# A hybrid decoder layer in float32: products and sums from GpSimd to VectorE, and the DeltaNet decay chain between two tiles of the RG-LRU

## The chip, the cores and the metric

The kernel runs on one core of a Trainium2 chip. The metric is the device time of one execution in microseconds, the median of several runs. Before the change it is 1122.11 us, the median of 3 runs (1121.78 to 1124.39).

## What is computed

One layer (depth 1) of a recurrent decoder, for a prompt of 512 tokens and 8 samples of 8 tokens, 576 columns together; the model width is 1024. Cut to what matters here:

```
h = rmsnorm(x); proj = h @ w_in
rg_x, rg_gate, s5_u, qkv, z, a_in, b_in, gate_logits = split(proj)
y_rg = (linear_scan(a, inp) * gelu(rg_gate)) @ w_o          # RG-LRU, width-4 conv before it
y_s5 = glu(gelu(Re(C s) + D u)) @ w_o                       # complex diagonal state space
# gated DeltaNet, 4 heads of 128: width-4 conv, silu, normed q and k
g    = -exp(a_log) * softplus(a_in + dt_bias); beta = sigmoid(b_in)
gc   = cumsum(g) in each chunk; decay = exp(gc_i - gc_j)
T    = inverse(I + strict(beta k k^T * decay)); u = T (beta v); w = T (beta k exp(gc))
v_new = u - w S; o = (q exp(gc)) S + (q k^T * decay) v_new; S = S exp(g_last) + k_dec^T v_new
y_gd = (rmsnorm(o) * silu(z)) @ w_o
mixed = sum_b sigmoid(gate_b) * y_b
x = x + rmsnorm(mixed @ w_out)
x = x + rmsnorm((silu(hf @ w_gate) * (hf @ w_up)) @ w_down),  hf = rmsnorm(x)
```

The outputs are y and the new states of the three branches, for the prompt and for each sample.

## The kernel before

All activations lie transposed, features on the 128 partitions and the 576 columns free, in two halves of 288. Each large product is made of three passes in a reduced format: weights and activations are split into a high and a low part, and high·high, high·low and low·high are summed in PSUM (`mm_part`, lines L199, L200, L201; in the last stage L1379 to L1381). A weight piece of 128x512 comes from HBM into `wr` (two buffers, line L170, on SP's queue), ACT makes its high part `wh` (L181), VectorE its low part `wl` (L182); four buffers of each. Activations are split in the same way (L236, L237).

The program is a list of tiles written in Python; a scheduler gives every engine its order of instructions, by the order in which they are written and by when buffers and operands are free in its own timeline. Each engine then works through its queue in that order and waits at each instruction for what it needs. Buffers matter: the big products go through three PSUM buffers `mm`, small ones through three `sm` and two `sr`; gates, merges and squares through a pool `T`; the 512 KB of sample states of a head, `s0` (`s` in the profile), through one buffer, so that the load of the next head's (L1159, SP's queue) follows the store of the one before (L1187).

The stages in order, with the names that the steps below use:

- The first norm and its split into `hh`, `hl` (line L374 in the second half); S5's tables and chunks (`s5_front`, `s5_chain`; products L699 and L700 into `s5yp`); the four tiles of the RG-LRU (`rg`), each with a convolution (L420 is one tap of such a convolution, L407 ACT's copy into the padded tile `pad`).
- Merge gates (`gate`, L788) and merges (`merge`): product with the branch's output weights, times the gate (L802, into `mg` or `mt`), from the second branch on added to the sum `mg` (L804, 128x576 on GpSimd). S5's GLU adds its parts in L822.
- The decay chain: a projection to 16 rows (`abps`, L849), transposes (`abc`), softplus and exponentials in some 50 small VectorE operations up to `gcl` (L871), cumulative sums on PE (`gcps`, L873 to L878), `bgp` (L901), a way through HBM (`bgd`).
- DeltaNet, two heads at a time: q, k, v (`gdn_qkv`, its `sqp` L931), `gdn_prep` (decay matrices `dt`, L973 to L983, products `kp` L994), `gdn_blk` (the inverse of 16x16 blocks by 15 steps on VectorE; L1032, L1036, L1064, L1067), `gdn_inv` (larger blocks by products `yp`, `pp`; L1078, L1081), `gdn_run` (the prompt's chunks, `tps`, `stp`, VectorE's `vk` L1124), `gdn_smp` (the samples: `zq` L1165, `s0` times the decay L1166, `zt` L1168, transposition L1169, `rrs` L1171, product L1172, `vns` L1174, L1175, masked copies `vm` L1180, product `up` L1183, sum L1184) and `gdn_outs` (norms of the heads: `cps`, L1197, the steps of a reciprocal root L112 to L118, `rows` L1204, L1206).
- After the last merge (gdn_wo), the product with w_out and its norm (squares summed in L1288, residual sum L1305), the feed-forward with 22 blocks (`ar`, L1331), and the last norm (squares summed in L1437, L1441 the scaled product, L1442 the residual sum, L1443 the output's DMA, eight of each in a half).

The scheduled order around the change is set by where the tiles are written:

Of the kernel before, what the change touches and what calls it, by code (L numbers as in the profile page):

```python
# [18 lines left out]
NT = 576  # L19
# [46 lines left out]
def hybrid_step(ctx: ExitStack, tc: tile.TileContext, i, o, dbg=None):  # L66
# [304 lines left out]
    def x_h(half):  # L371
        for k in range(KT):
            t = R("h")[:, :NH]
            (G if half and k % 4 == 3 else V).tensor_tensor(t, xa[:, k, hsl(half)], rw_[half], op=OP.mult)  # L374
            split(t, h[k][0][:, hsl(half)], h[k][1][:, hsl(half)])
# [415 lines left out]
    def merge(name, b, y, perm=False, ms=range(8), gates=()):  # L791
        for m in ms:
# [10 lines left out]
            if b:  # L803
                G.tensor_tensor(acc[m], acc[m], dst[:, :NT], op=OP.add)  # L804
# [5 lines left out]
    def s5_glu():  # L810
# [5 lines left out]
        for m in range(4):  # L816
# [5 lines left out]
            G.tensor_tensor(y[:, :NT], yh.bitcast(F32), yo.bitcast(F32), op=OP.add)  # L822
# [10 lines left out]
    rg_h = [rg(m) for m in range(3)]  # L833
    rg_h.append(rg(3))
    g1 = [gate(0, m) for m in range(5)]
# [70 lines left out]

    DQ.dma_start(o["rg_h"], hout)
# [56 lines left out]
    def gdn_prep(hd, st_):  # L964
# [14 lines left out]
        G.tensor_tensor(dt, dt, tri[:, None, :].to_broadcast([128, 4, 128]), op=OP.mult)  # L979
        G.tensor_tensor(dts, dts, C("tris")[:64], op=OP.mult)  # L980
        bt4 = bet[:, 0:NP].rearrange("p (n c) -> p n c", n=4)
        G.tensor_tensor(bt4, bt4, dt, op=OP.mult)
        G.tensor_tensor(bet[:64, NP:NT], bet[:64, NP:NT], dts, op=OP.mult)  # L983
# [25 lines left out]
        G.tensor_tensor(kqe[:, 1, :], kqe[:, 1, :], eg, op=OP.mult)  # L1009
# [14 lines left out]
    def gdn_blk(hds):  # L1024
# [3 lines left out]
        for e, hd in enumerate(hds):  # L1028
# [3 lines left out]
            G.tensor_tensor(t, st_["nq"][:, :, 0, :].rearrange("p n (b f) -> p n b f", f=16),  # L1032
# [3 lines left out]
            G.tensor_tensor(ts, st_["nqs"][:, 0, :].rearrange("p (b f) -> p b f", f=16),  # L1036
# [20 lines left out]
        for e, hd in enumerate(hds):  # L1057
# [9 lines left out]
            G.tensor_tensor(st_["nqs"][:, 0, :].rearrange("p (b f) -> p b f", f=16),  # L1067
# [6 lines left out]
    def gdn_inv(hd):  # L1074
# [3 lines left out]
        G.tensor_tensor(nl, nmat, lvl[:, None, :].to_broadcast([128, 4, 128]), op=OP.mult)  # L1078
# [77 lines left out]
    def gdn_smp(hd, st_):  # L1156
# [9 lines left out]
        G.tensor_tensor(s0, s0, egls[:, hd, :, None].to_broadcast([128, 8, 128]), op=OP.mult)  # L1166
# [11 lines left out]
        for a in range(2):  # L1178
            vm = GG("vm", 4, 128)[:64]
            G.tensor_tensor(vm, vn[:, None, :].to_broadcast([64, 4, 128]),  # L1180
# [102 lines left out]
    def add_sq(name, ss, src, last):  # L1283
# [4 lines left out]
        (V if last else G).tensor_tensor(ss, ss, sq, op=OP.add)  # L1288
        return ss

    for half in range(2):
# [10 lines left out]
        for m in range(8):  # L1302
            xv = x1[m][:, sl]
            V.scalar_tensor_tensor(xv, xv, P("g_post")[:, m:m + 1], rows, op0=OP.mult, op1=OP.mult)
            (V if m in (5, 7) else G).tensor_tensor(xv, xv, xr[m][:, sl], op=OP.add)  # L1305
# [117 lines left out]
    for half in range(2):  # L1423
        sl = hsl(half)
        prev, marks[:] = marks[:], []
        for m in range(KT):
# [9 lines left out]
            elif m < 7:  # L1436
                (V if half and m > 3 else G).tensor_tensor(ss, ss, sq, op=OP.add)  # L1437
        rows = norm_rows(tp2, [ss, sq], 1.0 / D, 4 * EPS)
        for m in range(8):
            xv = mx[m][:, sl]  # L1440
            V.scalar_tensor_tensor(xv, xv, P("g_postff")[:, m:m + 1], rows, op0=OP.mult, op1=OP.mult)  # L1441
            (V if half and m in (3, 5, 7) else G).tensor_tensor(xv, xv, x1[m][:, sl], op=OP.add)  # L1442
# [141 lines left out]
```

## Time and profile before

| | |
|---|---|
| median of 3 runs | 1122.11 us (1121.78 to 1124.39) |
| profiled execution | 1126.14 us |
| its span | 1124.4 us, 20031 instructions |
| TensorE's granted clock, mean | 0.974 |
| PE, VectorE, ACT, GpSimd busy | 1065.3, 714.6, 414.6, 176.9 us |
| HBM traffic | 89.05 MB read, 8.24 MB written |

The profiled execution is one of the program on the chip. Its span runs from the first to the last recorded instruction; the execution's own time is some 1.7 us longer. A busy time is what the engine's instructions took; a wait is put down to the instruction that ended last before it. PEclk is the granted clock of TensorE as a share of full speed, 1.0 or 0.5 at any one time.

### The profile page before, as it was taken

The page shows a single profiled execution, that of the slowest core. Times are in us where ns is not written, and L with a number is a line of the kernel's source. Part 1 is how long each engine was busy: PE and PEld are TensorE (multiplying, and loading weights), DVE is VectorE, ACT ScalarE, POOL GpSimd, SP SyncE. Part 2 cuts the span into 40 slices and gives each one's busy share as a digit, 9 for nine tenths or more (in the row PEclk, how much of TensorE's full clock was granted, in tenths as well). Part 3 has the DMA queues.
Part 4 walks back from the last instruction along what each step waited for, and adds up shares of the span by engine and source line. Part 5 has one row for each costly group of instructions (what it writes and reads, how often), then busy time and mean ns, then how long its engine had stood idle before and what let it go on. Part 6 is the DMA issues. An engine that isn't in the chain of part 4 may idle for free.

```text
span 1124.4 us, 20031 instructions
## 1 busy us (share of the span) xinstructions
PE 1065.3 (95%) x7874; PEld 1019.3 (91%) x7874; DVE 714.6 (64%) x1698; ACT 414.6 (37%) x847; POOL 176.9 (16%) x247
## 2 busy tenths in 40 slices
PE   6999999968999999999999998999999999999995
PEld 4899989967989889997989998899999999999994
DVE  8899989858977688546358377552344344443346
ACT  4368843425434432222334353343322222322211
POOL 1012111204532252221004231000000000000014
PEclk9999999978999999999999999999999999999997
DMA  6323224331322242222113514142222322213002
GB/s 199 107 83 101 79 80 110 91 93 53 111 86 79 84 136 63 74 95 76 57 53 122 178 57 131 57 146 80 77 94 76 94 76 82 87 57 94 1 1 85
DMA packets 61744, 98.59 MB, mean 88 GB/s; under 512 B 26570, under 2 KB 34898, under 8 KB 61650
## 3 DMA queue, kind: packets, MB, share of 16 engines
q1 hardware_dynamic: 61650, 97.31, 28.2%
q8 instruction: 62, 1.02, 0.4%
q14 instruction: 32, 0.26, 0.1%
HBM read 89.05 MB, written 8.24 MB: 87 GB/s over the span
## 4 chain that ended last, share of the span: by engine, by line
PE 82%; DVE 10%; DMA 4%; issue 2%; ACT 2%; POOL 0%; SPq 0%; DVEq 0%; ACTq 0%
PE mm L199 19%; PE mm L201 19%; PE mm L200 19%; PE mm L1381 4%; PE mm L1379 4%; PE mm L1380 4%; PE mm L381 2%; DVE wl L182 2%; DMA xa<-in_x 1%; PE up L1183 1%; PE rows L262 1%; PE gps L748 1%; PE s5yp L700 1%; DVE bu L1053 1%; PE s5yp L699 1%
## 5 line engine op out<-in xcount | busy, mean ns | idle before, releaser
L182 DVE TENSOR_TENSOR wl<-wr,wh 128x512 fp32r<-128x512 f32 x268 | 195.5, 734 | 171.9 <-ACT wh L181 164.9
L181 ACT ACTIVATE wh<-wr 128x512 fp32r<-128x512 f32 x268 | 166.3, 629 | 375.1 <-PE mm L200 226.4
L199 PE MATMUL mm<-hh,wh 128*128 128x288 f32 x768 | 233.0, 304 | 6.7 <-ACT pad L407 5.4
L200 PE MATMUL mm<-hl,wh 128*128 128x288 f32 x768 | 231.4, 301 | 0.0
L201 PE MATMUL mm<-hh,wl 128*128 128x288 f32 x768 | 230.1, 300 | 0.0
L199 PE MATMUL mm<-hfh,wh 128*128 128x288 f32 x704 | 208.7, 297 | 2.3 <-DVE ar L1331 1.9
L201 PE MATMUL mm<-hfh,wl 128*128 128x288 f32 x704 | 208.5, 297 | 0.0
L200 PE MATMUL mm<-hfl,wh 128*128 128x288 f32 x704 | 208.1, 296 | 0.0
L199 PEld LDWEIGHTS mm<-hh,wh 128*128 128x128 f32 x768 | 145.9, 190 | 12.7 <-ACT pad L407 5.6
L201 PEld LDWEIGHTS mm<-hh,wl 128*128 128x128 f32 x768 | 146.1, 190 | 2.8 <-issue 2.2
L200 PEld LDWEIGHTS mm<-hl,wh 128*128 128x128 f32 x768 | 146.1, 190 | 2.5 <-issue 1.7
L199 PEld LDWEIGHTS mm<-hfh,wh 128*128 128x128 f32 x704 | 133.5, 190 | 2.7 <-DVE ar L1331 2.2
L200 PEld LDWEIGHTS mm<-hfl,wh 128*128 128x128 f32 x704 | 133.6, 190 | 0.2 <-DVE hfl L237 0.2
L201 PEld LDWEIGHTS mm<-hfh,wl 128*128 128x128 f32 x704 | 133.4, 190 | 0.0
L1381 PE MATMUL mm<-fh,wl 128*128 128x288 f32 x352 | 104.0, 295 | 0.0
L1379 PE MATMUL mm<-fh,wh 128*128 128x288 f32 x320 | 94.5, 295 | 0.0
L1380 PE MATMUL mm<-fl,wh 128*128 128x288 f32 x320 | 94.3, 295 | 0.0
L199 PE MATMUL mm<-brh,wh 128*128 128x288 f32 x224 | 67.4, 305 | 4.3 <-DVE mg L802 1.9
L1437 POOL TENSOR_TENSOR fs<-fs,fs 128x288 f32<-128x288 f32 x9 | 7.3, 806 | 400.9 <-ACT fs L1433 400.9
L200 PE MATMUL mm<-brl,wh 128*128 128x288 f32 x224 | 68.2, 305 | 0.9 <-DVE brl L237 0.6
L201 PE MATMUL mm<-brh,wl 128*128 128x288 f32 x224 | 66.9, 299 | 0.0
L1381 PEld LDWEIGHTS mm<-fh,wl 128*128 128x128 f32 x352 | 66.1, 188 | 0.0
(464 smaller groups left out, 1905.5 us busy)
## 6 DMA issues: line engine op xcount, KB each, us to landing
wr<-in_w_in SPq DMA_DIRECT2D x48, 512.0 KB, 3.6
wr<-in_w_gate SPq DMA_DIRECT2D x22, 512.0 KB, 3.5
wr<-in_w_up SPq DMA_DIRECT2D x22, 512.0 KB, 3.6
wr<-in_w_down SPq DMA_DIRECT2D x20, 512.0 KB, 3.6
wr<-in_w_out SPq DMA_DIRECT2D x8, 512.0 KB, 3.5
xa<-in_x SPq DMA_DIRECT2D x8, 288.0 KB, 6.2
xr<-in_x SPq DMA_DIRECT2D x4, 576.0 KB, 8.1
out_y<-xr SPq DMA_DIRECT2D x16, 144.0 KB, 1.8
```

The lines of the kernel that those rows point to most:

```text
L181: S.activation(hi, raw, AF.Copy)
L182: (eng or lo_eng()).tensor_tensor(lo, raw, hi.bitcast(F32), op=OP.subtract)
L199: PE.matmul(acc, hi[:, k, :], xh[:, sl], start=k0 + k == 0, stop=False)
L200: PE.matmul(acc, hi[:, k, :], xl[:, sl], start=False, stop=False)
L201: PE.matmul(acc, lo[:, k, :], xh[:, sl], start=False, stop=k0 + k == n - 1)
L262: m0 = PE.matmul(rows[:, 96 * b:96 * b + 96], rc[:96, b:b + 1].to_broadcast([96, 128]), ident[:96, :96], start=True, stop=True).ins
L381: PE.matmul(ps, uw[m][k], xa[:, k, hsl(half)], start=k == 0, stop=k == KT - 1)
L699: PE.matmul(ypv[:, b_, :], tm[:, g, :], x[:, g, :], start=True, stop=False)
L700: PE.matmul(ypv[:, b_, :], cl[g // 4][:, g % 4, 1:9, :].rearrange("p d h -> p (d h)"), st[:, g, :], start=False, stop=True)
L1379: PE.matmul(acc, hi[:, k0 + k, :], xh, start=k == 0, stop=False)
L1380: PE.matmul(acc, hi[:, k0 + k, :], xl, start=False, stop=False)
L1381: PE.matmul(acc, lo[:, k0 + k, :], xh, start=False, stop=k == len(x) - 1)
```

## The change

116 operations of two tensors (17 lines) go from GpSimd to VectorE: the split norm product (L374), the merge sums (L804), S5's GLU sum (L822), DeltaNet's masks and decays (L979 to L983, L1009, L1032, L1036, L1067, L1078), the samples' decay and masked copies (L1166, L1180), and the sums of the later norms (L1288, L1305, L1437, L1442). GpSimd keeps copies and memsets. And the tiles of the RG-LRU are written in two pairs, with the decay chain between them and the first merge gates behind the second pair. Each line of the new kernel from here on has a number up to two lower than before (the decay chain) or the same. Cut to the lines that change:

```diff
@@ -371,7 +371,7 @@
     def x_h(half):
...
             t = R("h")[:, :NH]
-            (G if half and k % 4 == 3 else V).tensor_tensor(t, xa[:, k, hsl(half)], rw_[half], op=OP.mult)
+            V.tensor_tensor(t, xa[:, k, hsl(half)], rw_[half], op=OP.mult)
...
     def x_u(half, m, after=None):
@@ -801,7 +801,7 @@
...
             if b:
-                G.tensor_tensor(acc[m], acc[m], dst[:, :NT], op=OP.add)
+                V.tensor_tensor(acc[m], acc[m], dst[:, :NT], op=OP.add)
@@ -819,7 +819,7 @@
...
             yh, yo = yl[m]
-            G.tensor_tensor(y[:, :NT], yh.bitcast(F32), yo.bitcast(F32), op=OP.add)
+            V.tensor_tensor(y[:, :NT], yh.bitcast(F32), yo.bitcast(F32), op=OP.add)
@@ -830,9 +830,7 @@
...
     DQ.dma_start(o["s5"], s5o)
-    rg_h = [rg(m) for m in range(3)]
-    rg_h.append(rg(3))
-    g1 = [gate(0, m) for m in range(5)]
+    rg_h = [rg(m) for m in range(2)]
@@ -904,6 +902,8 @@
...
+    rg_h += [rg(m) for m in range(2, 4)]
+    g1 = [gate(0, m) for m in range(5)]
@@ -976,11 +976,11 @@
...
         S.activation(eg, eg, AF.Exp)
-        G.tensor_tensor(dt, dt, tri[:, None, :].to_broadcast([128, 4, 128]), op=OP.mult)
-        G.tensor_tensor(dts, dts, C("tris")[:64], op=OP.mult)
+        V.tensor_tensor(dt, dt, tri[:, None, :].to_broadcast([128, 4, 128]), op=OP.mult)
+        V.tensor_tensor(dts, dts, C("tris")[:64], op=OP.mult)
         bt4 = bet[:, 0:NP].rearrange("p (n c) -> p n c", n=4)
-        G.tensor_tensor(bt4, bt4, dt, op=OP.mult)
-        G.tensor_tensor(bet[:64, NP:NT], bet[:64, NP:NT], dts, op=OP.mult)
+        V.tensor_tensor(bt4, bt4, dt, op=OP.mult)
+        V.tensor_tensor(bet[:64, NP:NT], bet[:64, NP:NT], dts, op=OP.mult)
@@ -1006,7 +1006,7 @@
...
         V.tensor_tensor(nqs[:, 1], kpv[:, 1], dts, op=OP.mult)
-        G.tensor_tensor(kqe[:, 1, :], kqe[:, 1, :], eg, op=OP.mult)
+        V.tensor_tensor(kqe[:, 1, :], kqe[:, 1, :], eg, op=OP.mult)
@@ -1029,11 +1029,11 @@
...
             t = GG("nl", 4, 8, 16)
-            G.tensor_tensor(t, st_["nq"][:, :, 0, :].rearrange("p n (b f) -> p n b f", f=16),
+            V.tensor_tensor(t, st_["nq"][:, :, 0, :].rearrange("p n (b f) -> p n b f", f=16),
...
             ts = gp.tile([64, 4, 16], F32, name=nm("cms"), tag="cms")
-            G.tensor_tensor(ts, st_["nqs"][:, 0, :].rearrange("p (b f) -> p b f", f=16),
+            V.tensor_tensor(ts, st_["nqs"][:, 0, :].rearrange("p (b f) -> p b f", f=16),
@@ -1064,7 +1064,7 @@
...
                                 bd[:, None, :, None].to_broadcast([128, 4, 8, 16]), op=OP.mult)
-            G.tensor_tensor(st_["nqs"][:, 0, :].rearrange("p (b f) -> p b f", f=16),
+            V.tensor_tensor(st_["nqs"][:, 0, :].rearrange("p (b f) -> p b f", f=16),
@@ -1075,7 +1075,7 @@
...
         nl = GG("nl", 4, 128)
-        G.tensor_tensor(nl, nmat, lvl[:, None, :].to_broadcast([128, 4, 128]), op=OP.mult)
+        V.tensor_tensor(nl, nmat, lvl[:, None, :].to_broadcast([128, 4, 128]), op=OP.mult)
@@ -1163,7 +1163,7 @@
...
             PE.matmul(zqv[:, b], s0[:, b, :], kqe[:, :, c0:c0 + 8], start=True, stop=True)
-        G.tensor_tensor(s0, s0, egls[:, hd, :, None].to_broadcast([128, 8, 128]), op=OP.mult)
+        V.tensor_tensor(s0, s0, egls[:, hd, :, None].to_broadcast([128, 8, 128]), op=OP.mult)
@@ -1177,7 +1177,7 @@
...
             vm = GG("vm", 4, 128)[:64]
-            G.tensor_tensor(vm, vn[:, None, :].to_broadcast([64, 4, 128]),
+            V.tensor_tensor(vm, vn[:, None, :].to_broadcast([64, 4, 128]),
@@ -1285,7 +1285,7 @@
...
             return sq
-        (V if last else G).tensor_tensor(ss, ss, sq, op=OP.add)
+        V.tensor_tensor(ss, ss, sq, op=OP.add)
@@ -1302,7 +1302,7 @@
...
             V.scalar_tensor_tensor(xv, xv, P("g_post")[:, m:m + 1], rows, op0=OP.mult, op1=OP.mult)
-            (V if m in (5, 7) else G).tensor_tensor(xv, xv, xr[m][:, sl], op=OP.add)
+            V.tensor_tensor(xv, xv, xr[m][:, sl], op=OP.add)
@@ -1434,12 +1434,12 @@
...
             elif m < 7:
-                (V if half and m > 3 else G).tensor_tensor(ss, ss, sq, op=OP.add)
+                V.tensor_tensor(ss, ss, sq, op=OP.add)
...
             V.scalar_tensor_tensor(xv, xv, P("g_postff")[:, m:m + 1], rows, op0=OP.mult, op1=OP.mult)
-            (V if half and m in (3, 5, 7) else G).tensor_tensor(xv, xv, x1[m][:, sl], op=OP.add)
+            V.tensor_tensor(xv, xv, x1[m][:, sl], op=OP.add)
...
```

The scheduler gives new orders. Three places follow; a row is line, operation, output<-inputs and size, and the number at the end of a name is the buffer's, the same in both orders.

PE in the sample step of head 3 (`zq`, the states `s`, `up`) and the norm rows of heads 0 and 1. Before, around the transposition L1169:

```order
L201 MATMUL mm_6154<-hh_127,wl_6146 128x288
L199 MATMUL mm_6154<-hh_129,wh_6145 128x288
L1169 MATMUL zq_5323<-con,zt_5333 64x128
L200 MATMUL mm_6154<-hl_130,wh_6145 128x288
L201 MATMUL mm_6154<-hh_129,wl_6146 128x288
```

Big products (here for the gate z) stand on both sides of it, in each of its steps. In the changed kernel, all that stands from `zq` to the first `rows`:

```order
L1165 MATMUL zq_5323<-kqe_4553,s_944_5315 128x16 x8
L1123 MATMUL tps_6302<-con,kqe_4553 128x128
L1169 MATMUL zq_5323<-con,zt_5333 64x128
L1123 MATMUL tps_6338<-con,v_819_4789 128x128
L1172 MATMUL zq_5323<-rrs_5336,nqs_4870 64x128
L1175 MATMUL zq_5323<-nqs_4870,vns_5339 128x64
L1183 MATMUL up_5345<-vm_5343,vk_5318 128x512
L1123 MATMUL tps_6356<-con,v_785_4550 128x128
L1183 MATMUL up_5350<-vm_5348,vk_5318 128x512
L1204 MATMUL rows_6232<-rs_va_6217,con 128x288
```

Before, 22 big products stood between L1165 and L1169, 23 more before L1172, 17 more before L1175 and 58 more before the rows; now there are none. On PE the chains of DeltaNet as a whole stand 117 to 156 big products later than before.

VectorE at the same place in the changed kernel (`vm` are the masked copies, `rs_va` and `rs_yt` the norm's root, `vk` the scaled transposes of the next chunks):

```order
L1166 TENSOR_TENSOR s_944_5315<-s_944_5315,egls 128x1024
L1124 TENSOR_SCALAR vk_6303<-tps_6302,kdc 128x128
L1171 SCALAR_TENSOR_TENSOR rrs_5336<-zq_5323,begc,vk_5318 64x128
L1180 TENSOR_TENSOR vm_5343<-vns_5339,con 64x512
L1180 TENSOR_TENSOR vm_5348<-vns_5339,con 64x512
L1197 TENSOR_TENSOR rs_va_6217<-cps_6208,ssq_3008 128x288
L1176 TENSOR_TENSOR v_819_4789<-zq_5323,zt_5333 128x64
L112 TENSOR_SCALAR rs_va_6217<-rs_va_6217 128x288
L113 TENSOR_SCALAR rs_yt_6218<-rs_va_6217 128x288
L114 TENSOR_SCALAR rs_yt_6218<-rs_yt_6218 128x288
L1184 TENSOR_TENSOR s_944_5315<-s_944_5315,up_5345 128x512
L116 TENSOR_TENSOR rs_va_6217<-rs_yt_6218 128x288
```

L1166 and L1180 stood on GpSimd's queue; the norm's first sum L1197 stands behind both `vm` now. Before, L1197 stood behind splits and `zs` sums of the gates.

PE where the decay chain's result is used first, `gcps`. Before:

```order
L700 MATMUL s5yp_1333<-st_1299,cl_1161 128x72
L699 MATMUL s5yp_1333<-s5x_1108,tm_1117 128x72
L700 MATMUL s5yp_1333<-st_1299,cl_1161 128x72
L873 MATMUL gcps<-gcl,con 128x16
L874 MATMUL gcps<-gcl,con 64x4
```

In the changed kernel:

```order
L700 MATMUL s5yp_1333<-st_1299,cl_1161 128x72
L699 MATMUL s5yp_1333<-s5x_1108,tm_1117 128x72
L700 MATMUL s5yp_1333<-st_1299,cl_1161 128x72
L871 MATMUL gcps<-gcl,con 128x16
L872 MATMUL gcps<-gcl,con 64x4
```

The products of the chain's end stand where they stood; `abps`, its beginning, stands some 480 instructions further ahead.

## Rows read from the trace of the kernel before

**Rows 1.** The page: busy time by engine, and the chain's shares by engine.

```profile
PE 1065.3 (95%) x7874; PEld 1019.3 (91%) x7874; DVE 714.6 (64%) x1698; ACT 414.6 (37%) x847; POOL 176.9 (16%) x247
...
PE 82%; DVE 10%; DMA 4%; issue 2%; ACT 2%; POOL 0%; SPq 0%; DVEq 0%; ACTq 0%
```

**Rows 2.** PE's waits: total us, times, longest us.

```profile
PE gcps L873 <- DVE gcl L871: 7.1, 1, 7.1
PE mm L199 <- ACT pad L407: 5.4, 1, 5.4
PE yp L1081 <- DVE tu L1064: 2.0, 1, 2.0
...
PE mm L199 <- DVE mg L802: 1.9, 1, 1.9
...
PE mm L199 <- DVE mt L802: 1.5, 1, 1.5
PE mm L199 <- ACT glt L819: 1.4, 2, 1.1
...
PE mm L200 <- DVE ml L237: 0.9, 1, 0.9
```

**Rows 3.** GpSimd's groups, by form: busy us, mean ns, idle before.

```profile
L804 POOL TENSOR_TENSOR mg<-mg,mt 128x576 f32<-128x576 f32 x16 | 27.7, 1731 | 120.9 <-DVE mt L802 90.7 <-DVE mt L799 20.5 <-DVE bt L1051 9.7
```

**Rows 4.** VectorE's largest group; timelines of VectorE and GpSimd (start, us), two stretches.

```profile
L182 DVE TENSOR_TENSOR wl<-wr,wh 128x512 fp32r<-128x512 f32 x268 | 195.5, 734 | 171.9 <-ACT wh L181 164.9 <-PE mm L200 0.9
...
605.76 1.29 DVE L182 TENSOR_TENSOR wl<-wr,wh 128x512 fp32r<-128x512 f32 x2 [1.76 <-ACT wh L181]
...
611.49 2.52 DVE L182 TENSOR_TENSOR wl<-wr,wh 128x512 fp32r<-128x512 f32 x2
...
610.98 1.88 POOL L804 TENSOR_TENSOR mg<-mg,mt 128x576 f32<-128x576 f32 x1 [1.59 <-DVE mt L802]
...
253.45 2.60 DVE L420 SCALAR_TENSOR_TENSOR cv<-pad,par,cv 128x600 f32<-128x600 f32 x2
...
255.98 1.55 DVE L973 TENSOR_SCALAR dt<-eg,gc 128x128 f32<-128x128 f32 x1
```

**Rows 5.** PE's timeline (start, us), 494 to 505 us.

```profile
494.69 1.12 PE L1183 MATMUL up<-vm,vk 64*128 64x512 f32 x2
...
500.75 0.29 PE L199 MATMUL mm<-hh,wh 128*128 128x288 f32 x1
...
504.60 0.29 PE L201 MATMUL mm<-hh,wl 128*128 128x288 f32 x1
```

**Rows 6.** VectorE's timeline, 494 to 531 us.

```profile
495.85 0.69 DVE L1184 TENSOR_TENSOR s<-s,up 128x512 f32<-128x512 f32 x1 [0.64 <-PE up L1183]
...
517.19 0.46 DVE L1197 TENSOR_TENSOR rs_va<-cps,ssq 128x288 f32<-128x288 f32 x1
...
518.38 0.31 DVE L114 TENSOR_SCALAR rs_yt<-rs_yt 128x288 int32<-128x288 int32 x1
...
520.81 0.46 DVE L117 TENSOR_TENSOR rs_va<-rs_va 128x288 f32<-128x288 f32 x1
```

**Rows 7.** SP's queue: issue of the sample states' load L1159; its time to landing.

```profile
499.27 0.33 SPq L1159 DMA_DIRECT2D s<-in_gdn_s  x1
...
DMA to landing us min/median/max: 3.4/3.5/5.9
```

**Rows 8.** Busy us by window: PE, PEld, DVE, ACT, POOL (instructions), PEclk, DMA share.

```profile
494.69:528.70 34.01, 34.01 (x235) 29.52 (x233) 17.57 (x41) 8.34 (x17) 4.38 (x3) 1.00 0.29 103
...
338.00:342.00 4.00, 3.98 (x19) 4.00 (x20) 3.96 (x5) 1.89 (x5) 2.66 (x5) 0.57 0.60 142
600.00:622.00 22.00, 19.05 (x140) 18.36 (x139) 19.98 (x28) 10.23 (x18) 10.26 (x6) 1.00 0.51 153
270.00:310.00 40.00, 38.50 (x272) 35.91 (x272) 38.01 (x94) 18.80 (x38) 15.75 (x15) 1.00 0.29 95
```

**Rows 9.** VectorE's timeline at the end.

```profile
1118.90 1.88 DVE L1442 TENSOR_TENSOR xr<-xr,x 128x288 f32<-128x288 f32 x3
```


## The prediction, made before the changed kernel was run

> **What bounds the kernel now.** I read the page's busy shares and its chain first [rows 1]. PE is busy for 95% of the span and carries 82% of the chain that ended last; GpSimd is 16% busy and 0% of the chain. So the reader is to see that no time is won by making GpSimd's work shorter as such. Time is won or lost only where PE stands still, or runs at its lower clock after it stood still. The next view is therefore the list of PE's waits [rows 2]: the change touches the gcps wait (7.1 us), the pad wait (5.4), the block wait on tu (2.0) and the waits at the two ends of the merges (mg 1.9; mt 1.5 and ml 0.9). The third view is the timeline of the stretch in which the states of the last head's samples and the norms of heads 0 and 1 are made [rows 5 to 7]: there PE does not wait at all, because big products stand between the small ones, and that is what the new order takes away.
>
> The profiled execution took 1126.14 us (span 1124.4), 4.0 us above the median of the runs, 1122.11. I make the sum as a difference within this execution and add it to the median.
>
> **The change, part by part.**
>
> *Moved operations.* 116 operations leave GpSimd, some 129 us of its time by the groups of its view; the largest is the merge sum L804, 16 at 1731 ns [rows 3]. On VectorE the nearest row is L1184 (128x512, 0.69 us, [rows 6]); by size, 24 of 128x576 at 0.75, 16 of 128x512 and 8 of 64x512 at 0.69, 4 of 128x1024 at twice 0.69, 48 of 128x288 at 0.45 and 16 small ones at 0.24 make about 66 us more work. Against it, VectorE is held up now wherever GpSimd works beside it: two L182 took 1.29 us alone and 2.52 beside an L804 [rows 4]. L182 alone is 268 operations at a mean of 734 ns; at the 690 that an undisturbed one shows, 12 us are hold-ups. So VectorE goes from 715 us to some 750 to 780, still far under the span. A page of the Trainium skill says it more sharply (SBUF — State Buffer, Who interferes with whom): a VectorE instruction with two SBUF inputs and a GpSimd instruction that reads SBUF block each other wholly, the first one holds the port. The trace agrees as far as [rows 4] go. By it alone the change would be a gain; that is the first rival.
>
> *Where the decay chain stands.* The abps projection moves forward by some 480 instructions on PE, but gcps, the first product that needs the chain's result, stands behind the last s5yp in both orders, at the same place, since the three small PSUM buffers are held by the S5 products until then. So the 7.1 us are not won. Between the abt copy and gcl VectorE now has three more L420 and one more L182 (some 3 us), which stood ahead of it before; I take 0.5 us for it, between 0 and 2.2.
>
> *The pad wait (5.4 us).* L979, L980, L982 and L983 of head 0 now stand on VectorE ahead of the last L420, on which ACT's pad, and PE behind it, wait: 0.6 + 0.3 + 0.6 + 0.2, 1.7 us, and some 1.5 us of steps moved ahead with them, 3.2 together. Against it stand 2.6 us of hold-ups that go: two L420 took 2.60 us, and one L973 1.55, beside GpSimd's L979 and L982 [rows 4]. I take +0.6, between -0.5 and +1.5.
>
> *First merges (158 to 165 us).* VectorE's order has the S5 steps L674, L681 and L682 ahead of the first brl, and PE reaches the merge without the abps products that filled it. Before, mg cost 1.9 us here; I take +0.8, between -1 and +2.5.
>
> *Block chain of heads 0 and 1.* L1081 waited 2.0 us for tu, and the clock was at 0.57 on average behind it [rows 8]; one stretch at the lower level costs about 1.7 us. In the new order 117 big products more stand ahead of L1081 on PE, 15 us, and VectorE's added work up to there is near what it loses in hold-ups. I take all of it: -2.0 - 1.7. The glt wait (1.4 us) sits where VectorE is 95% busy; more work and fewer hold-ups cancel there: 0, between -1.4 and +2.
>
> *Last merges (600 to 622 us).* VectorE is busy for 20.0 of 22 us [rows 8]. It gains six sums of 0.67 and loses about as much in hold-ups [rows 4], but the sum no longer takes 1.9 us on the path from mt to mh and ml. Of the waits mt 1.5 and ml 0.9, and a shorter one on mh, I take half: -1.5, between 0 and -3.0.
>
> *The bare stretch.* This is the largest term, and it comes from the order. All four heads' chains slide back against the big products by 117 to 156 of them, while the products at the end of the stretch (gates of the third branch) cannot come earlier: they wait for T buffers that heads 0 and 1 free. Before, from the last up of head 2 (494.69) to rows (528.70) PE was busy for all of 34.0 us [rows 8], with 186 big products; in the new order the same two marks have 30 between them, and from zq on there is none. The big products start 0.133 us apart (30 from 500.75 to 504.60, [rows 5]), so 156 of them are 20.8 us of cover, and 13.2 us of PE's own work stay. What is the chain worth without cover?
>
> - Up to zq: from up to the load's issue 4.6 us (494.69 to 499.27), 3.5 us to land [rows 7]: 8.1. In the new order one weight load stands between the store and this load on SP's queue, so 9 to 9.5. PE has 8.9 us of work there (up 1.1, [rows 5], two pairs of cps 1.4, 30 products 4.0, nine transposes 2.4). Idle some 0.5.
> - From zq's end to rows, VectorE in its order (in the section on the change): L1166 twice 0.69, vk and rrs 0.34 each, L1172 on PE 0.43, vns on ACT 0.36, two vm 1.38, then L1197 to L114 1.5 (517.19 to 518.69), L1184 0.69, three steps of 0.48, L1184 0.69, six steps of 0.48 [rows 6]: 11.4. PE's work in it is L1169, three transposes, L1172, L1175 and two up, 4.2. Idle 7.2.
>
> So PE stands still for about 8 us where it stood for none. At least 5: without the neighbours on VectorE's queue (second vm, two L1184, vk: 2.4 us) 11.4 falls to 9.0. At most 11: the load 3.5 us later, behind the weights. L1166 and L1180 are now themselves on VectorE's part of that chain. The clock falls after a stall of that length as it did after gcps; a dip stood at 533 us already, so I take 1.0 more, between 0 and 3.4.
>
> *Tail.* Behind the last rows, GpSimd did five of the eight sums beside VectorE's eight L1441, and VectorE three behind them, from 1118.90 to 1120.78 [rows 9]. Now all eight sums follow the eight L1441 on one queue: the first ends near 1119.4, the last near 1122.0 instead of 1120.8, and the output's DMAs with them: +1.0, between 0.3 and 2.4. The other norm sums (L1288, L1305, L1437, L374) end no PE wait, but the cps wait at 1107 us, where three sums more and no hold-ups meet: nothing.
>
> **Sum.** 0.5 + 0.6 + 0.8 + 8.0 + 1.0 + 1.0 = +11.9; -2.0 - 1.7 - 1.5 = -5.2. Net +6.7, so 1122.1 + 6.7 = **1128.8 us**. With the bounds taken as independent this case reaches from 1124.4 to 1134.2.
>
> **Rivals.**
>
> *Relief wins (faster).* VectorE, free of GpSimd, is early everywhere. For it: [rows 4], and the waits on VectorE in [rows 2]. Then the pad wait loses its 2.6 us, glt 1.4, the last merges 3.0, the block chain 3.7, and the clock's stretch at the lower level behind the pad wait half of its cost, 1.7: -12.4; the bare stretch at its least +5.0, the tail +1.0: 1122.1 - 6.4 = 1115.7 us. It decides if the bare stretch costs under 5. Against it: most hold-ups lie where PE does not wait. The page of the skill named above stands behind this rival.
>
> *The bare stretch is bought back elsewhere (same).* The bare stretch costs what the sum says, but the relief's terms that the sum doesn't hold come too (pad 2.6, glt 1.4, the other half of the merges 1.5, the clock 1.7: 7.2): 1128.8 - 7.2 = 1121.6 us.
>
> *VectorE is the bound from 260 to 310 us (slower).* From 270 to 310 it is busy for 38.0 of 40 us, beside 15.8 of GpSimd [rows 8], nearly all of it moved: at 0.75 for 1.73 that is 6.8 us more. If no hold-up went, 44.8 us would have to fit into 40, and PE would wait for wl: 1128.8 + 4.8 = 1133.6 us.
>
> That the chain moves and gcps with it is out by the order.
>
> **How the numbers follow.** Forecast 0.58, relief 0.22, bought back 0.10, VectorE the bound 0.10. A measurement of this kernel can tell some 0.3%, 3.4 us: slower is above 1125.5, faster below 1118.7. The forecast's own low end (0.06) is within that, of relief 0.07 is too: faster 0.15, same 0.06 + 0.07 + 0.10 = 0.23, slower 0.62. The range leaves out half of relief below and the end of the bound case above: 1116.5 to 1135.
>
> **What would show it.** In the new profile: a wait of PE for rows, vm or rrs of 5 to 11 us in sum, near 510 us, that wasn't there; gcps at 7 us again; no wait of L1081; L182 near a mean of 690 ns; the last L1442 near 1122 us of the span's scale. The forecast is wrong if PE has other products in that stretch, or if the chain from zq to rows takes under 8 us; and the size is wrong if new waits for wl stand between 260 and 310 us.

## The result: 0.8% slower, about as forecast, with some terms off

| | before | after |
|---|---|---|
| median | 1124.68 us (8 runs, 1121.78 to 1129.01) | 1133.8 us (8 runs, 1129.1 to 1136.89) |
| ratio | | 1.0077, 95% interval 1.005 to 1.0103 |
| profiled execution | 1126.14 us, span 1124.4 | 1136.68 us, span 1134.9 |
| TensorE's granted clock, mean | 0.974 | 0.959 |

The forecast was +6.7 us and 1128.8 (1116.5 to 1135.0); measured were +9.1 in the medians and +10.5 between the two profiled spans. The eight executions of either kernel spread over 7 to 8 us, and the profiled one of the kernel before lies 1.5 us above its median; so times are compared by medians, and a profile tells where the time lies.

The page of the changed kernel: busy time by engine, the chain that ended last, and VectorE's largest group. They answer to [rows 1] and the first of [rows 4].

```profile
PE 1069.7 (94%) x7874; PEld 1024.4 (90%) x7874; DVE 736.0 (65%) x1814; ACT 415.0 (37%) x847; POOL 66.6 (6%) x131
...
PE 87%; DVE 7%; DMA 3%; ACT 1%; issue 1%; SPq 0%; DVEq 0%; ACTq 0%
...
L182 DVE TENSOR_TENSOR wl<-wr,wh 128x512 fp32r<-128x512 f32 x268 | 183.0, 687 | 154.4 <-ACT wh L181 143.0
```

GpSimd lost 110 us of busy time and VectorE gained only 21 net, since L182 alone gave 12.5 back (734 to 687 ns). The hold-ups of VectorE were real, and they went, on L182 the 12 us that were forecast. Yet PE is no less busy than before, and the kernel is slower. PE's waits in the changed kernel, to be held against [rows 2]:

```profile
PE rows L262 <- DVE rs_o L118: 12.3, 4, 4.6
...
PE gcps L871 <- DVE gcl L869: 6.7, 1, 6.7
PE mm L199 <- ACT pad L407: 4.6, 1, 4.6
PE rows L1204 <- DVE rs_va L118: 3.7, 1, 3.7
PE cps L255 <- DVE fs L1437: 3.0, 1, 3.0
PE mm L200 <- DVE brl L237: 2.7, 2, 2.5
...
PE tps L1123 <- DVE vk L1124: 1.5, 4, 0.8
PE sqp L931 <- ACT sq L952: 1.5, 1, 1.5
PE cps L255 <- DVE sqx L1288: 1.5, 1, 1.5
```

The waits for tu, glt and mt are gone, as the relief would have it. New are the 3.7 us for rows L1204 (the last head's samples), the wait for sqx, and one for brh (1.4, in the first merges). Longer are those for tps (1.5 for 0.9), for brl (the first merges, 2.7 for 0.6), for fs (3.0 for 1.7) and for rows L262 of the norms (12.3 for 9.9). Now the stretch that the prediction's largest term speaks of: PE's timeline (start, us), VectorE's, and one window (columns as in [rows 8]):

```profile
519.82 3.30 PE L1165 MATMUL zq<-kqe,s 128*128 128x16 f32 x16 [0.29 <-DMA s<-in_gdn_s]
...
524.70 0.48 PE L1123 MATMUL tps<-con,v 128*128 128x128 f32 x1 [0.79 <-DVE vk L1124]
...
526.25 0.68 PE L1175 MATMUL zq<-nqs,vns 64*128 64x64 f32 x2 [0.45 <-ACT vns L1174]
527.05 2.04 PE L1183 MATMUL up<-vm,vk 64*128 64x512 f32 x2
...
535.20 1.33 PE L1204 MATMUL rows<-rs_va,con 1*128 1x288 f32 x4 [3.70 <-DVE rs_va L118]
```

```profile
523.16 1.23 DVE L1166 TENSOR_TENSOR s<-s,egls 128x1024 f32<-128x1024 f32 x1 [3.76 <-PE zq L1165]
...
526.23 1.29 DVE L1180 TENSOR_TENSOR vm<-vns,con 64x512 f32<-64x512 f32 x2 [1.33 <-ACT vns L1174]
```

```profile
520.20:544.10 23.90, 17.86 (x55) 11.31 (x55) 15.66 (x34) 4.13 (x11) 0.00 (x0) 0.50 0.06 23
```

From zq to rows no big product runs, PE waits at four of the steps, and the granted clock is at its lower level (0.50) for 23.9 us. In the kernel before, PE had no wait in this chain, and the lower level stood at 532.8 to 536.2 only. The lower level stretches the chain's own products: `up` takes 2.04 us a pair where it took 1.12 [rows 5].

### The profile page after: what moved, and what is told of

Read it like the earlier page. It is cut to its first block, busy times and chain, and to the rows that moved or that the text cites. A ratio compares the mean times of both kernels' runs of the same rounds, so it can differ in the third digit from the quotient of the medians.

```text
span 1134.9 us, 19962 instructions
## 1 busy us (share of the span) xinstructions
PE 1069.7 (94%) x7874; PEld 1024.4 (90%) x7874; DVE 736.0 (65%) x1814; ACT 415.0 (37%) x847; POOL 66.6 (6%) x131
## 4 chain that ended last, share of the span: by engine, by line
PE 87%; DVE 7%; DMA 3%; ACT 1%; issue 1%; SPq 0%; DVEq 0%; ACTq 0%
PE mm L199 20%; PE mm L200 20%; PE mm L201 20%; PE mm L1381 4%; PE mm L1379 4%; PE mm L1380 4%; PE mm L381 2%; DMA xa<-in_x 1%; DVE wl L182 1%; PE up L1183 1%; PE rows L262 1%; PE gps L748 1%; PE zq L1165 1%; PE kp L994 1%; DMA wr<-in_w_out 1%
## 5 line engine op out<-in xcount | busy, mean ns | idle before, releaser
L182 DVE TENSOR_TENSOR wl<-wr,wh 128x512 fp32r<-128x512 f32 x268 | 183.0, 687 | 154.4 <-ACT wh L181 143.0
L199 PEld LDWEIGHTS mm<-hh,wh 128*128 128x128 f32 x768 | 146.3, 191 | 10.2 <-ACT pad L407 4.8
L1380 PEld LDWEIGHTS mm<-fl,wh 128*128 128x128 f32 x320 | 60.1, 188 | 0.0
```

The source lines that it names most:

```text
L182: (eng or lo_eng()).tensor_tensor(lo, raw, hi.bitcast(F32), op=OP.subtract)
L199: PE.matmul(acc, hi[:, k, :], xh[:, sl], start=k0 + k == 0, stop=False)
L1380: PE.matmul(acc, hi[:, k0 + k, :], xl, start=False, stop=False)
```

## The experiments

Twelve kernels, in four groups of four, four, two and two: the first four of the table; mg, gdn_only and the two holds; the two pins; m_blk and m_smp. In each group the kernel before ran on the same chip; its median was 1123.57 (17 runs), 1124.04 (23), 1124.49 (12) and 1125.38 us (18).

| kernel | what moves | median us (runs) | ratio to before, 95% |
|---|---|---|---|
| o_only | the decay chain only | 1129.37 (6) | 1.0053 (1.0034 to 1.0073) |
| e_only | all operations, no chain | 1126.15 (12) | 1.002 (1.0007 to 1.0033) |
| norms_only | the norms' operations | 1129.26 (5) | 1.0046 (1.0028 to 1.0064) |
| merge_only | L804, L822 | 1112.78 (5) | 0.9905 (0.9888 to 0.9923) |
| gdn_only | the DeltaNet operations | 1123.29 (12) | 0.9987 (0.9974 to 0.9999) |
| mg | merges and DeltaNet | 1122.94 (12) | 0.9991 (0.9979 to 1.0003) |
| m_blk | merges and block inverse | 1117.4 (7) | 0.9933 (0.9908 to 0.9957) |
| m_smp | merges and samples | 1120.71 (12) | 0.9962 (0.9943 to 0.998) |
| merge_hold | merge_only, one gate held back | 1117.1 (6) | 0.9937 (0.9915 to 0.9959) |
| after_hold | the change, one gate held back | 1135.44 (4) | 1.0102 (1.0086 to 1.0118) |
| mg_pin | mg, five products held back | 1133.75 (7) | 1.0083 (1.0051 to 1.0115) |
| after_pin | the change, five products held back | 1141.33 (4) | 1.0151 (1.0123 to 1.0179) |

### The change taken apart

**o_only**: the kernel before with the chain's move alone.

```diff
-    rg_h = [rg(m) for m in range(3)]
-    rg_h.append(rg(3))
-    g1 = [gate(0, m) for m in range(5)]
+    rg_h = [rg(m) for m in range(2)]
...
+    rg_h += [rg(m) for m in range(2, 4)]
+    g1 = [gate(0, m) for m in range(5)]
```

> The order alone: the decay chain stands between the second and third tile of the RG-LRU, every operation stays on the engine it had before. By the theory of cover (PE loses time only where small products have no big ones between them) the DeltaNet part has the order of before and costs nothing; what is left is the first merge of the S5 part near 158 us, which has lost the abps products that stood in it: waits of PE there of 5 to 6 us instead of 2.4, and a longer stretch at the lower clock, so +4 to +6 us. If the loss of the whole change came from VectorE's added work alone, this run would be within 1 us of before.

**e_only**: all 17 lines moved to VectorE, the chain where it was, that is the change without the diff just shown.

> The engines alone: all 116 operations on VectorE, the decay chain written where it was before. By the theory of cover the bare stretch is there in full (no big product between zq and rows), some 7 us with the clock, the norm sums cost some 4 (1.5 near 660 us, 1.2 and 1.4 at the end), the block chain and the last merges give back 3.7 and 2.5: +5 us together. If the order of the decay chain were what makes the bare stretch, PE would have no wait for rows near 530 us here, and the run would be 1 to 2 us faster than before.

**norms_only** and **merge_only**: these lines alone (L374, L1288, L1305, L1437, L1442, and L804, L822).

```diff
-                G.tensor_tensor(acc[m], acc[m], dst[:, :NT], op=OP.add)
+                V.tensor_tensor(acc[m], acc[m], dst[:, :NT], op=OP.add)
...
-            G.tensor_tensor(y[:, :NT], yh.bitcast(F32), yo.bitcast(F32), op=OP.add)
+            V.tensor_tensor(y[:, :NT], yh.bitcast(F32), yo.bitcast(F32), op=OP.add)
```

> Only the sums of the norms (L374, L1288, L1305, L1437, L1442) go to VectorE, 50 operations. By the theory of cover they stand on the path at three places without cover: a wait of PE on the sum of squares near 660 us (+1.5), the same at the last norm (+1.2), and the last sums behind the last rows (+1.4): +4 us. By the theory of relief (VectorE is no longer held up by GpSimd) it is 0 to 2 us faster.

> Only the merge sums (L804) and the sums of the S5 GLU (L822) go to VectorE, 20 operations of 128x576, the largest moved. In this order big products stand between all steps of the last head's samples, so by the theory of cover there is no bare stretch, the last merges lose 2.5 us of waits and L1081 its 2.0 us and the clock behind it: 4 to 6 us faster than before. If added work on VectorE as such were what costs, this run would be about 1 us slower.

The chain's move costs 5.8 us, as expected. The norms cost 5.7, more than expected, all the engines together 2.6, half of what was expected. The merges alone win 10.8, twice what was expected of them, and are faster than either kernel of the case. The chain's 5.8 and all the engines' 2.6 together make 8.4 of the 9.1 measured. In merge_only PE's waits for glt, tu, mt and ml are gone and L182 is at 698 ns:

```profile
L182 DVE TENSOR_TENSOR wl<-wr,wh 128x512 fp32r<-128x512 f32 x268 | 185.8, 698 | 157.5 <-ACT wh L181 149.7
...
PE gcps L873 <- DVE gcl L871: 7.1, 1, 7.1
PE mm L199 <- ACT pad L407: 4.2, 1, 4.2
PE cps L255 <- DVE fs L1437: 2.4, 1, 2.4
...
PE rows L1204 <- DVE rs_va L118: 0.6, 1, 0.6
```

In norms_only L182 keeps its 735 ns, so nothing is won, while PE has the wait for fs to pay (1.7 before) and a new one for sqx; another of 0.9 us at rows L262 (1102 us) is new too:

```profile
L182 DVE TENSOR_TENSOR wl<-wr,wh 128x512 fp32r<-128x512 f32 x268 | 195.7, 735 | 166.9 <-ACT wh L181 159.8
...
PE cps L255 <- DVE fs L1437: 3.0, 1, 3.0
...
PE cps L255 <- DVE sqx L1288: 1.5, 1, 1.5
```

### Two parts that do no harm alone

**gdn_only** moves L979 to L983, L1009, L1032, L1036, L1067, L1078, L1166 and L1180; **mg** these and the two merge lines; the edit is `G.` to `V.` in each.

> The DeltaNet operations alone on VectorE, the merges and norms left on GpSimd, the decay chain where it was. By the order TensorE keeps some 90 big products between zq of head 3 and rows, so no bare stretch. Theory A (cost comes from order, and relief counts only where TensorE waits): pad about 1 less or more, the wait for tu (2.0 and its clock) gone, glt as before: 2 to 4 us less than before, 0.996 to 0.999. Rival B (the DeltaNet operations cost by their length in VectorE's chain, wherever the products stand): 3 to 8 us more, 1.003 to 1.007.

> The merges (L804, L822) and the DeltaNet operations (L979 to L983, L1009, L1032, L1036, L1067, L1078, L1166, L1180) on VectorE, the norms' sums and products left on GpSimd, the decay chain where it was. Theory A (parts add; the DeltaNet operations together with the merges slide the chains of all heads behind the big products): as with all engines moved, less the norms' +5.7, that is 1120.5 us, ratio 0.996 to 0.999, with the bare stretch's waits of 5 to 7 us near 515 to 530 us. Rival B (the norms' sums make the bare stretch, the DeltaNet operations are free or a gain): no bare stretch and 1110 to 1113 us, as with the merges alone or better.

The DeltaNet operations alone win 0.8 us, the merges alone 10.8; together they should win 11.5, and they win 1.1. The 10.4 us that are missing lie in the bare stretch and close around it. By PE's timelines merge_only and mg are level up to the 1400th big product (it starts at 314.76 and 314.82 us). At the 2500th, just behind the rows, they are 10.8 us apart, and at the end of the span 11.3. Between the two marks (first merge_only, then mg) PE stands still for 2.5 us and for 7.3, and the mean clock is 0.99 and 0.95:

```profile
314.76:529.56 214.80, 212.27 (x1707) 195.03 (x1706) 152.32 (x375) 71.12 (x157) 49.25 (x73) 0.99 0.28 88
...
314.82:540.41 225.59, 218.33 (x1708) 198.62 (x1707) 165.09 (x415) 70.81 (x157) 12.29 (x36) 0.95 0.28 84
```

By the order, zq of head 3 stands at the 2383rd big product in merge_only, at the 2380th in gdn_only, and at the 2472nd in mg, which is the last one that PE can have before rows. The first `rows` comes in merge_only at 519.01 us, in mg at 527.81 (PE's timelines, one row of each; then mg's window):

```profile
519.01 0.76 PE L1204 MATMUL rows<-rs_va,con 1*128 1x288 f32 x4 [0.62 <-DVE rs_va L118]
```

```profile
527.81 1.33 PE L1204 MATMUL rows<-rs_va,con 1*128 1x288 f32 x4 [3.71 <-DVE rs_va L118]
```

```profile
513.60:537.50 23.90, 17.87 (x55) 11.32 (x55) 15.68 (x34) 4.13 (x11) 0.00 (x0) 0.50 0.06 23
```

Nearly the same waits and the same 23.9 us at the lower level as in the changed kernel, with the decay chain in its old place. So the chain's move has no part in the bare stretch: o_only has at rows L1204 only the 0.3 us for `v` that the kernel before has, and none for rs_va. The norms' sums and the chain's move cost their 5.7 and 5.8 elsewhere; mg, with the bare stretch in full, is no slower than the kernel before.

**m_blk** and **m_smp** add to the merges the operations ahead of yp alone, or L1166 and L1180 alone.

> The merges on VectorE and of the DeltaNet operations only those of the block inverse (L1032, L1036, L1067, L1078), which stand ahead of yp; all else as before. By the order zq of head 3 stands at the 2425th big product, so 47 of them are left as cover up to rows: between the merges alone (89 left, 1112.8 us) and merges with all DeltaNet operations (none left, 1122.9 us). Theory A (the cost is a threshold: idle time and the lower clock come only where the cover ends, and 47 products of 0.133 us, 6.3 us, with the 4.2 us of TensorE's own work nearly hold the 11 us from zq to rows): rows within 2 us of the merges alone, 1112 to 1116 us, 0.989 to 0.993. Theory B (each moved operation costs in proportion to VectorE's added work): 3 to 5 us over the merges alone, 1116 to 1118 us, 0.993 to 0.995.

> The merges on VectorE and of the DeltaNet operations only those of the samples (L1166, L1180), which stand in the chain from zq to rows itself; all else as before. By the order 56 big products are left as cover from zq of head 3 to rows, but none behind the two up. Theory A (threshold): as in the run before, 1112 to 1116 us, 0.989 to 0.993, with a wait for rows of under 2 us. Theory B (the longer chain from zq to rows is what costs, the work ahead of it nothing): most of the 10 us between the merges alone and merges with all DeltaNet operations is here: 1118 to 1123 us, 0.995 to 0.999, and the run with the block inverse stays at 1113.

The threshold that I expected isn't there. Both have a wait for rows (PE's timelines, m_blk's first), and their ratios, 0.9933 and 0.9962, lie between the 0.9905 of the merges alone and the 0.9991 of mg: part of the cover lost is part of the time lost. The lower level behind zq lasts 10.2 us in both, against 3.4 in merge_only and 23.9 in mg. m_smp keeps more cover than m_blk (56 products for 47) and is yet the slower one by the medians, so the length of the chain from zq to rows counts too; but the two intervals overlap, as m_blk's does with that of the merges.

```profile
519.70 1.33 PE L1204 MATMUL rows<-rs_va,con 1*128 1x288 f32 x4 [4.99 <-DVE rs_va L118]
```

```profile
526.72 1.33 PE L1204 MATMUL rows<-rs_va,con 1*128 1x288 f32 x4 [3.83 <-DVE rs_va L118]
```

### Giving the cover back by force

Is the scheduler's order alone to blame, or does VectorE's added work make the chain late? In **after_hold** and **merge_hold** the z gate of head 3 waits in PE's order for zq of head 3, so that its products stand behind it:

```diff
-        ps = w_in(IDX["z"] + hd)
+        ps = w_in(IDX["z"] + hd, after={0: zq_mark[3]} if hd in (3,) else None)
```

> The changed kernel with one thing more: the 16 products of head 3's z gate (L1211) are held back on TensorE until zq (L1165) of head 3 has been given out, so that about 100 big products stand between zq and rows of the last head again, as in the kernel before, instead of none; engines and order are otherwise those of the change. Theory A (the bare stretch costs time because the chain lost its cover): the waits between 517 and 539 us of the changed kernel (rrs, L1175, vm, rows 3.7; 6.1 us in sum) fall to under 2, and the lower clock of 520 to 544 us shrinks or goes; but the way from up of head 2 by s0 store and load to zq of head 3 (8.1 us, TensorE's own work there 4 to 5) stands bare in turn for 2 to 4 us. In sum 2 to 6 us less than the changed kernel: ratio to the kernel before 1.002 to 1.006. Rival B (the stretch is only where the time shows, VectorE's added work is the cause): the waits come back in another place, and the ratio stays at 1.007 to 1.009.

> The merges alone on VectorE (0.9905 of the kernel before), and head 3's z gate held back behind zq of head 3 as in the first run of this call, so that the cover between zq and rows is that of the kernel before (120 big products instead of 89). If small waits near 517 to 522 us (2.2 us in sum) are for want of cover, they go: 1 to 3 us less, 0.988 to 0.990. If the held products lack elsewhere, same or up to 2 us more: 0.990 to 0.993.

The waits behind zq fall from 5.8 to 0.9 us in after_hold, and one of 5.43 us stands ahead of zq instead, for the DMA of the samples' states, with 23.9 us at the lower level around it (timeline, window; zq has line 1167 here). The time is no better. In merge_hold the same wait takes 2.0 us, and the median is 4 us worse than without the hold, with intervals that just overlap.

```profile
510.95 3.60 PE L1167 MATMUL zq<-kqe,s 128*128 128x16 f32 x16 [5.43 <-DMA s<-in_gdn_s]
```

```profile
495.60:519.50 23.90, 16.96 (x84) 12.81 (x84) 6.23 (x14) 1.04 (x3) 1.50 (x3) 0.50 0.16 62
```

In **mg_pin** and **after_pin** five products wait for marks all along the second pair of heads, which sets zq of heads 2 and 3 to the 2136th and the 2352nd big product:

```diff
-        ps = w_in(IDX["gate"] + 8 * b + m)
+        ps = w_in(IDX["gate"] + 8 * b + m, after=hold('yp2' if (b, m) == (1, 7) else None))
...
-        ps = w_in(IDX["z"] + hd)
+        ps = w_in(IDX["z"] + hd, after=hold({0: 'zq2', 1: 'up20', 2: 'up21', 3: 'zq3'}.get(hd)))
```

> Merges and DeltaNet operations on VectorE, norms on GpSimd, decay chain where it was (as in mg, 0.9991 of the kernel before), and five big products held back behind marks of the second pair of heads: the gate of the last s5 merge behind yp (L1081) of head 2, the z gates of heads 0 to 3 behind zq of head 2, the two up of head 2 and zq of head 3. On TensorE zq of heads 2 and 3 then stand at the 2136th and 2352nd big product instead of the 2326th and the 2472nd, near where the kernel before has them (2171 and 2352), with 120 products from zq to rows. Theory A (the scheduler's order alone takes the cover away; VectorE has room enough to serve the chain early): no waits of 3 to 4 us near 510 to 540 us, no lower clock of 24 us there, and the time of the merges alone: 1110 to 1116 us, 0.988 to 0.993. Rival B (VectorE's added work makes the chain late whatever the order): TensorE waits for tu at yp of head 2, or for zq, by 5 to 15 us near 445 to 470 us, and the time stays at 1120 to 1128 us, 0.997 to 1.004.

> The changed kernel with the same five products held back behind the same marks. Theory A: the changed kernel without its bare stretch, that is 8 to 10 us less than it: 1123 to 1127 us, 0.999 to 1.003; what is left over the kernel before are the norms and the first merges. Rival B: 1130 to 1140 us, with a wait of 5 us or more for tu at yp of head 2.

Rival B's wait came, and the times are worse than it said: PE stands 6.1 us for tu ahead of yp of head 2 (line 1086 here), in mg_pin as in after_pin, then 1.9 and 2.0 us ahead of zq, and both are 7 to 11 us slower than without the pins.

```profile
468.80 2.08 PE L1086 MATMUL yp<-tu,nl 128*128 128x128 f32 x8 [6.06 <-DVE tu L1069]
```

So the chain itself is late. VectorE makes the tu of the second pair from 449.01 us on in merge_only, from 464.36 in mg (VectorE's timelines of merge_only, mg and mg_pin, where the line is 1069):

```profile
449.01 0.69 DVE L1064 TENSOR_TENSOR tu<-cu,con 128x512 f32<-128x512 f32 x1 [1.86 <-DMA cu<-ub]
...
464.36 0.69 DVE L1064 TENSOR_TENSOR tu<-cu,con 128x512 f32<-128x512 f32 x1 [0.99 <-DMA cu<-ub]
...
468.06 0.69 DVE L1069 TENSOR_TENSOR tu<-cu,con 128x512 f32<-128x512 f32 x1 [4.14 <-DMA cu<-ub]
```

From 420 to 460 us VectorE is busy for 37.1 of 40 us in mg and for 31.2 in merge_only. In mg_pin 4.1 of PE's 6.1 us are a time in which VectorE waits too, for the DMA that brings its own result, the block inverse, back from HBM. Of the places in PE's order that were tried for the chain of mg and of the changed kernel, the scheduler's late one did the least harm. The pins also crowd head 2's small products together, so how much of the loss is theirs stays open. A kernel that gives the chain precedence in VectorE's queue wasn't tried, so it isn't shown whether VectorE lacks the room or only serves the chain too late.

## Why the prediction was right, and where not

The direction, the range and the place of the largest stall came as forecast. That the sum came so near is luck, as the two profiled executions show when PE's timelines are cut at the same big products (us):

| stretch | before | after | difference | forecast |
|---|---|---|---|---|
| up to the 900th (first merges) | 210.99 | 217.53 | +6.5 | +0.8 |
| 900th to 1400th (gcps, pad, glt) | 106.24 | 104.45 | -1.8 | +1.1 |
| 1400th to 2500th (block chain, bare stretch, clock) | 222.64 | 225.45 | +2.8 | +5.3 |
| 2500th to 3100th (last merges) | 94.66 | 92.06 | -2.6 | -1.5 |
| 3100th to the end (norms, tail) | 489.84 | 495.41 | +5.6 | +1.0 |
| sum | 1124.37 | 1134.90 | +10.5 | +6.7 |

The loss against the kernel before stands mostly at the two ends, where the forecast had 1.8 us. The experiments say the same by medians: the chain's move +5.8, the norms +5.7, merges and DeltaNet operations together -1.1. The bare stretch is real, and it costs what those moves would have won.

**The bare stretch** (forecast +8.0, 5 to 11, and the clock +1.0, 0 to 3.4). The waits behind the last big product sum to 6.8 us in the trace, against 0.8 in the kernel before: within the range. The clock was mis-sized. I had one more short stretch at the lower level; the runs show 23.9 us for 3.4. What this costs is read from the products in it. PE's groups by form, first before, then after:

```profile
L1183 PE MATMUL up<-vm,vk 64*128 64x512 f32 x16 | 9.0, 641 | 0.0
L1165 PE MATMUL zq<-kqe,s 128*128 128x16 f32 x64 | 7.6, 253 | 0.0
...
L1204 PE MATMUL rows<-rs_va,con 1*128 1x288 f32 x16 | 4.2, 453 | 0.3 <-DVE v L1206 0.3
```

```profile
L1183 PE MATMUL up<-vm,vk 64*128 64x512 f32 x16 | 10.8, 763 | 0.1
L1165 PE MATMUL zq<-kqe,s 128*128 128x16 f32 x64 | 9.0, 279 | 0.3 <-DMA s<-in_gdn_s 0.3
L1204 PE MATMUL rows<-rs_va,con 1*128 1x288 f32 x16 | 5.3, 606 | 4.3 <-DVE rs_va L118 3.7 <-DVE v L1206 0.6
```

Three groups alone are 4.3 us longer; not all of it need be time lost, since PE waits for the chain behind some of these products. The whole difference between mg and merge_only in this stretch, waits and clock together, is 10.8 us, where the forecast had 9.0. The step "a dip stood at 533 us already, so I take 1.0 more" thus failed. The mechanism, no big products between zq and rows, is confirmed. The forecast's sign rested on it; but against the kernel before, the whole stretch from the 1400th to the 2500th product is only 2.8 us longer. The relief in it is larger than the block chain's 3.7: merge_only is 7.8 us shorter there (214.80), of which PE's waits are 2.6 and the dip at 338 us by the prediction's estimate 1.7; the rest stands in no wait of PE's list and stays open. That the stretch "comes from the order" needs a correction: the order is that of the scheduler, but it follows from merges and DeltaNet operations on VectorE together, not from the new place of the decay chain, and it goes with a chain that is late on VectorE. Nor did every head slide by 117 to 156 big products: zq of heads 0 to 3 moved by -12, 112, 155 and 120.

**First merges** (forecast +0.8, -1 to +2.5). Before, two waits summed to 2.4 us; now there are five with 6.1 in sum. So +3.7, above the range, and the lower clock lasts 10.2 us (158.4 to 168.6) instead of 3.4. PE's timeline there:

```profile
156.18 0.44 PE L699 MATMUL s5yp<-s5x,tm 128*128 128x72 f32 x2 [0.55 <-ACT X L650]
158.35 0.85 PE L199 MATMUL mm<-brh,wh 128*128 128x288 f32 x2 [1.41 <-ACT brh L236]
159.74 0.61 PE L199 MATMUL mm<-brh,wh 128*128 128x288 f32 x1 [0.54 <-ACT gt L788]
162.80 0.61 PE L200 MATMUL mm<-brl,wh 128*128 128x288 f32 x1 [2.46 <-DVE brl L237]
174.81 0.40 PE L199 MATMUL mm<-brh,wh 128*128 128x288 f32 x1 [1.18 <-DVE mg L802]
```

It is the chain's move that makes them: e_only has the two waits of before here, and o_only waits of the new kind (brh 0.9, gt 0.9, mg 2.1). I had named the mechanism (abps no longer fills the merge) and priced it far too low. Of o_only's 5.8 us in the medians the profiles show 0.5 in the span, since its profiled execution is the fastest of its six and that of the kernel before lies 2.6 above the median measured beside o_only. Up to the 900th big product o_only is 4.4 us later (215.39 for 210.99), and the dip at 338 us, which the kernel before has there, is missing from it. What the other executions of o_only lose, and where, is open.

**Norms** (tail forecast +1.0; "the other norm sums: nothing"). The tail was right: from the first L1441 to the end of the last L1442 [rows 9] it was 5.3 us, and it is 6.4 (VectorE's timeline; the L1441 began at 1115.50 before).

```profile
1124.60 3.49 DVE L1441 SCALAR_TENSOR_TENSOR xr<-xr,par,rows 128x288 f32<-128x288 f32 x8 [1.75 <-PE rows L262]
1128.00 3.03 DVE L1442 TENSOR_TENSOR xr<-xr,x 128x288 f32<-128x288 f32 x8
```

"Nothing" for the rest was wrong, and with the first merges it is the term that the sum had most wrong: the wait for sqx (1.5) is new, as is one of 0.9 at rows L262 (1108 us), and that for fs went from 1.7 to 3.0. They stand at the end of a sum on which PE waits, and no hold-up of L182 was relieved for it, as norms_only shows.

**gcps** stayed, as the order said (7.1 to 6.7; forecast +0.5, 0 to 2.2, so just outside). **Pad** fell by 0.8, forecast +0.6 within -0.5 to 1.5, so just outside. **Block chain**: the wait for tu (2.0) and its dip went, as forecast. The window 338 to 342, at 0.57 in [rows 8], is now

```profile
338.00:342.00 4.00, 4.00 (x33) 4.00 (x32) 3.66 (x15) 2.11 (x5) 0.85 (x4) 1.00 0.37 131
```

VectorE's busy time, 750 to 780 us by the forecast, is 736.0.

**Last merges**: mt 1.5 is gone and ml is at 0.2 for 0.9, so -2.2 for a forecast of -1.5. **glt** (1.4) went; forecast 0, with -1.4 as the bound.

**The rivals.** "Relief wins" was no idle fear: with the merges alone it is what happens, at 1112.8 us. (The 1115.7 worked out for it were for the whole change, with 5.0 of bare stretch in them, so that the two are near proves nothing.) It fails in the changed kernel because the other moves load VectorE where its chain is on the path. The Trainium skill's page "SBUF — State Buffer", section "Who interferes with whom", which stood behind this rival, says that a VectorE instruction with two SBUF inputs and a GpSimd instruction that reads SBUF exclude each other at a shared port. The trace agrees: L182, which reads `wr` and `wh`, goes from 734 to 698 ns when the merges leave GpSimd. It doesn't follow that every move pays: gdn_only has L182 at 699 and wins 0.8 us, norms_only leaves it at 735 and costs 5.7. "Bought back elsewhere" did not happen in the sum: against the forecast's terms pad gave back 1.4 of the 2.6 that it held, glt its 1.4 and the last merges 0.7 of 1.5, but the first merges and the norms took more. "VectorE the bound from 260 to 310" did not happen: none of PE's waits there is for wl.

The change came within 2.4 us of the forecast (+9.1 for +6.7) because errors of both signs met; the time itself is 5.0 off, since the median of before over more runs is 2.6 higher than the one shown ahead. Too small were the clock, the first merges and the norms' sums; on the other side glt, pad, the last merges and the stretch ahead of zq fell by more than the sum held.

## What to carry to other kernels

Price a moved operation by the chain it lands in, and then price the moves together: two sets that cost nothing or win alone took 10.4 us from each other here. Alone each left some 90 big products beside one latency chain, together they left none. And price the small sums at the ends as well: the norms' sums, taken at nothing but for the tail, cost 5.7 us. Where PE is 95% busy, count the big products that stand beside each chain up to the next barrier; when they run out, expect the stall and a long stretch at the lower clock behind it. Take the moves one set at a time: L804 and L822 alone give 1112.78 us, which beats both kernels of the case.

## What the runs showed that I had not expected

The stretch at the lower granted clock was 23.9 us in each of the changed kernel, mg and after_hold (20.5 in e_only), though PE's single waits in it were 5.4 us at most; the gcps wait of 7.1 us in the kernel before has 13.7 us (235.8 to 249.5) at the lower level around it. What they have in common is small products and waits; in each, big products come back only in the last 2 to 5 us.

Moving cover from one end of a chain to the other by holding a gate back moved the wait with it (5.8 us behind zq in the changed kernel became 5.4 ahead of it) and gave nothing back.
